# Cosine attention on one core: the norm sums of 36 pairs' Q taken by VectorE's statistics instruction, K scaled on GpSimd, a cubic in place of a quartic, and new engine orders

## The chip, the cores and the metric

One core of a Trainium2 chip runs the whole kernel. A core has five engines with an instruction queue each: TensorE (PE in the profile, its weight loads PEld), VectorE (DVE), ScalarE (ACT), GpSimd (POOL), and SyncE (SP), which here only issues DMAs. The metric is the device time of one execution in microseconds (us), the median of several runs. Every engine takes its instructions strictly in the order in which they were written for it, and a semaphore wait at the head of a queue holds back all that stands behind it.

## What is computed

For 8 batches x 12 heads, with 512 rows of 64 values each:

```python
Q_norm = Q / (np.linalg.norm(Q, axis=-1, keepdims=True) + 1e-10)
K_norm = K / (np.linalg.norm(K, axis=-1, keepdims=True) + 1e-10)
scores = np.einsum('bhqd,bhkd->bhqk', Q_norm, K_norm) / tau
weights = np.exp(scores - np.max(scores, axis=-1, keepdims=True))
weights = weights / (np.sum(weights, axis=-1, keepdims=True) + 1e-10)
return np.einsum('bhqk,bhkd->bhqd', weights, V)
```

With tau = 0.1 the scores lie between -10 and 10, so the kernel exponentiates without taking a maximum off. The sum of the weights is a 65th column of V that holds ones.

## The kernel before

The 96 heads are worked off as 48 **pairs** s = 0 to 47, two heads h each. Of Q and K a pair has 128 partitions x 8 rows (2 heads x 4 tiles t) x 64 values. Each pair goes through these steps; the name in capitals is the one under which the code registers the operation (`P.add`), and the line is the one that the profile shows:

- LD (L337), LV (L340): SP loads Q, K and V; a tile `qk` holds Q and K of a pair, 15 of them are in rotation.
- SQ (L366): GpSimd squares Q and K together, 128x1024, into `sq`, in bf16.
- SSQ (L396, L401) and RED (L410, L414, L418): the sum of 64 squares of each row. For the 40 pairs of `SUM_BOTH`, TensorE adds groups of columns with 16 matmuls by the identity, and VectorE reduces the 64 columns that remain to 16 sums in one instruction (L410). For the pairs of `BY_VECTOR` (35, 39, 43, 47), VectorE reduces all the squares itself with two 128x512 instructions (L418).
- NEW (L443, L447, L450): the reciprocal square root, by a bit trick and polynomial steps on small tiles, for a whole **group** of pairs at once (`GROUPS`: pairs 0 to 3 alone, 4 to 19 in groups of two, 20 to 47 in groups of four). Step 6 gives Q's factors, 7 K's factors for GpSimd, 8 K's factors for VectorE.
- SCL (L485): rows times factor, in bf16, into `qn`. Q is scaled on VectorE, K on VectorE for the 20 pairs of `K_ON_DVE` and on GpSimd for the others.
- TR (L494) and EVA (L512): TensorE transposes, VectorE copies the result from PSUM to `qt`. EVA is the last step ahead of the scores.
- SCO (L633) and EXP (L657): for each of 4 chunks c of 128 keys, TensorE computes 128x1024 scores into one of two PSUM buffers, and ScalarE takes their exponential into `et`. A score chunk must wait for the exponential of the chunk two before it.
- PV (L682), RCP (L701), NRM (L703), ST (L707): TensorE multiplies the weights by V (cast on GpSimd, VC, L665), VectorE takes the reciprocal of the 65th column and scales the output, SP stores it. The SSQ of a later pair uses a spare part of the same PSUM bank, between a pair's PV and its RCP.

Two chunks, (36, 3) and (45, 3) (`OFF`), don't go to ScalarE: VectorE cuts their scores (X, L573, L575) into a power of two and a rest, and GpSimd computes a polynomial of the rest (Y, L595, L596, L602, L603), 128x1024 at a time, six instructions each.

What sets the order: the table `ORDER` (from L814) lists for each engine, as numbers, the operations in the order in which the engine runs them. A number counts the `P.add` calls, which the code makes pair by pair. `Program.run` (L43) turns the needs of each operation into semaphore waits, and nothing is reordered on the chip. In this text RCP8.1 means RCP of pair 8, head 1.

The branch for `stats(s)` (L361, L378, L460) is in this version too, but `STATS_FROM = 99` turns it off. Its core:

```python
for h in range(2):
    rows = qk[iq][:, 0, h, :].rearrange("p (t d) -> p t d", t=NT)
    for t in range(0, NT, 2):
        last = e.bn_stats(out=st[...two groups of three...],
                          in_=rows[:, t : t + 2].rearrange("p t d -> p d t"))
```

One such instruction reads 128 values of f32 per partition, alternately from row t and from row t + 1, which lie 64 values apart, and gives count, mean and summed squared deviation of the even values (row t) and of the odd ones (row t + 1).

Of the kernel before, what the change touches and what calls it, by code (L numbers as in the profile page):

```python
# [108 lines left out]
def bass_cosine_similarity_attention_kernel(  # L109
# [200 lines left out]
    def stats(s):  # L310
        return s >= STATS_FROM and group[s] not in NORM_ON_ACT

# [10 lines left out]
    def pair(s):  # L323
# [6 lines left out]
        for w, x in ((0, Q), (1, K)):  # L330
            if s == 0:
                for h in range(2):
                    P.add(("LD", 0, w, h), "act" if w else "sp", "ldh", -1000 + h,  [],
                          lambda e, w=w, x=x, h=h: e.dma_start(out=qk[iq][:, w, h], in_=src(x, s)[:, h]), slot=f"head{w}_{h}")
                continue
            P.add(("LD", s, w), "sp", "ld1" if s == 1 else "ld", s, [*([("SCL", 0, w, 0), ("SCL", 0, w, 1), ("SQ", 0, w, 0), ("SQ", 0, w, 1)] if s == R_QK else [key("SCL", s - R_QK, w), *((squares(s - R_QK, w) if w or not stats(s - R_QK) else [("RED", s - R_QK, 0)]) if s >= R_QK else [])])],
                  lambda e, w=w, x=x: e.dma_start(out=qk[iq][:, w], in_=src(x, s)),  # L337
                  slot=f"first{s}_{w}" if s <= 3 else f"qk{iq}")
# [195 lines left out]
    def last_step(s, c):  # L534
        return 5 if (s, c) in OFF_ON_POOL + OFF_ON_BOTH else 4
# [18 lines left out]
    def poly(s, c, at):  # L554
# [4 lines left out]
        a0, a1, a2, a3, a4 = POLY_K if here else POLY  # L559
# [39 lines left out]
        if (s, c) in OFF_ON_POOL:  # L599
            k = cc ** 0.5  # L600
            steps = [("pool", "yt", mul(w, z, z)), ("pool", "ys", add(w, w, a1, k)),
                     ("pool", "ys", lambda e: e.tensor_scalar(out=z, in0=z, scalar1=a2 * cc, scalar2=a3 * cc, op0=ALU.mult, op1=ALU.add)),  # L602
                     ("pool", "yt", mul(w, w, w)), ("pool", "yt2", lambda e: e.tensor_tensor(out=w, in0=w, in1=z, op=ALU.add)),  # L603
                     ("pool", "yt3", mul(e_, w, p2))]
# [146 lines left out]
POLY = (-186.9751803485176, 100772.4799431421, -50373599.073513225, 207520169.07623482, 3.565140779347853e-11)  # L751
# [9 lines left out]
BY_VECTOR = (35, 39, 43, 47)  # L761
Q_ON_PE = ()
SUM_BOTH = (4, 5, 6, 7, 8, 9, 10, 11, 12, 13, 14, 15, 16, 17, 18, 19, 20, 21, 22, 23, 24, 25, 26, 27, 28, 29, 30, 31, 32, 33, 34, 36, 37, 38, 40, 41, 42, 44, 45, 46)
# [3 lines left out]
STATS_FROM = 99  # L767
# [8 lines left out]
JOINT_FROM = 0  # L776
OFF_ON_POOL = ((36, 3), (45, 3))
OFF_ON_BOTH = ()
X_ON_POOL = ()
K_ON_DVE = (1, 2, 3, 4, 9, 12, 15, 18, 21, 24, 27, 30, 33, 36, 39, 40, 42, 44, 46, 47)  # L780
# [29 lines left out]
def slack(s, most):  # L810
# [14 lines left out]
    ),  # L825
    "pool": (
# [7 lines left out]
    ),  # L834
    "dve": (
# [23 lines left out]
    ),  # L859
# [80 lines left out]
```

## Time and profile before

| what | value |
|---|---|
| median of 3 runs | 188.97 us (188.75 to 189.37) |
| profiled execution, first to last instruction (its span) | 186.8 us |
| what the median has beyond that span | 2.2 us |
| ScalarE (ACT) busy | 180.2 us, 210 instructions |
| VectorE (DVE) busy | 159.9 us, 523 instructions |
| GpSimd (POOL) busy | 165.7 us, 147 instructions |
| TensorE busy / weight loads busy | 179.5 us / 117.9 us, 3010 each |
| granted TensorE clock | 1.00 throughout |

The profile is that of one execution. "Busy" is the time in which at least one instruction of the engine runs; instructions of one engine can overlap, so on an engine whose instructions overlap the mean duration of one is more than the distance from one start to the next. Waits are attributed to what released them. The page gives for the profiled execution its span, no other time.

### The profile page before, as it was taken

Reading aid. Unit: us, or ns where it says so; the run is one execution under the profiler, and the core shown is the slowest. Engines: PE = TensorE matmul, PEld = TensorE weight load, DVE = VectorE, ACT = ScalarE, POOL = GpSimd, SP = SyncE. Lnnn points to the kernel's source line nnn. Section 1 sums busy time; section 2 is a strip of 40 time slices with the busy share of each in tenths; the row PEclk is TensorE's granted clock in tenths of the full one; section 3 lists DMA queues with packets and bytes.
Section 4 is the critical chain, followed back from the end, with each engine's and each line's share of the span. In section 5 each row is a group of like instructions: output and inputs, shape, how many; then the busy total and the mean of one; then the engine's idle time right before and its main releaser. Section 6 shows DMA issues by size and latency. Waiting matters only on the chain.

```text
span 186.8 us, 7242 instructions
## 1 busy us (share of the span) xinstructions
PE 179.5 (96%) x3010; PEld 117.9 (63%) x3010; DVE 159.9 (86%) x523; ACT 180.2 (96%) x210; POOL 165.7 (89%) x147
## 2 busy tenths in 40 slices
PE   7889999999999999999999999999999999998993
PEld 2456766666667666666676666766656566555653
DVE  2789998987987978979889988999999999998664
ACT  5799999999999999999999999999999999999992
POOL 3799999999989998999999899999999999907940
PEclk9999999999999999999999999999999999999999
DMA  5999999999999877999999999999798731113135
GB/s 158 354 349 351 349 358 329 288 351 364 370 376 369 283 245 230 309 303 307 312 379 367 328 371 335 319 312 298 241 303 294 239 105 56 60 56 116 60 112 168
DMA packets 52447, 50.79 MB, mean 272 GB/s; under 512 B 3136, under 2 KB 52416, under 8 KB 52416
## 3 DMA queue, kind: packets, MB, share of 16 engines
q1 hardware_dynamic: 51984, 50.02, 81.8%
q8 instruction: 23, 0.38, 0.8%
q10 hardware_dynamic: 432, 0.33, 0.5%
q14 instruction: 8, 0.07, 0.1%
HBM read 37.75 MB, written 12.58 MB: 269 GB/s over the span
## 4 chain that ended last, share of the span: by engine, by line
ACT 92%; PE 3%; DVE 2%; DMA 1%; POOL 0%; issue 0%; DVEq 0%
ACT et L657 91%; DMA qk<-in_K_dram 1%; PE oops L682 1%; PE scps L633 1%; DVE xs L260 1%; DVE ob L732 0%; POOL sq L256 0%; PE tps L283 0%; ACT ys L432 0%; DVE qn L273 0%; DVE ob L703 0%; PE oops L401 0%; ACT nps L435 0%; PE oops L281 0%; DVE rd L730 0%
## 5 line engine op out<-in xcount | busy, mean ns | idle before, releaser
L657 ACT ACTIVATE et<-scps 128x1024 bf16<-128x1024 f32 (+1 forms) x191 | 173.8, 1155 | 0.3 <-PE scps L633 0.3
L366 POOL TENSOR_TENSOR sq<-qk 128x1024 bf16<-128x1024 f32 x44 | 82.8, 1895 | 0.6 <-DMA qk<-in_K_dram 0.6
L633 PE MATMUL scps<-qt 64*128 64x512 bf16 x380 | 74.5, 386 | 2.2 <-ACT et L657 1.0
L682 PE MATMUL oops<-vb,et 128*128 128x65 bf16 x1504 | 75.8, 194 | 0.1
L682 PEld LDWEIGHTS oops<-vb,et 128*128 128x128 bf16 x1504 | 57.0, 98 | 27.7 <-issue 21.9
L485 DVE TENSOR_TENSOR qn<-qk,nps 128x512 bf16<-128x512 f32 x67 | 44.2, 678 | 0.7 <-ACT nps L435 0.6
L703 DVE TENSOR_TENSOR ob<-oops,rd 128x256 f32<-128x256 f32 x94 | 39.5, 422 | 1.7 <-DVE ys L447 0.2
L512 DVE COPY qt<-tps 128x1024 bf16<-128x1024 bf16 x47 | 32.3, 687 | 3.9 <-PE tps L494 3.0
L494 PE MATMUL tps<-ident,qn 128*128 128x128 bf16 x376 | 34.3, 220 | 0.6 <-DVE qn L485 0.6
L485 POOL TENSOR_TENSOR qn<-qk,rk 128x512 bf16<-128x512 f32 x27 | 28.1, 1045 | 2.6 <-DVE rk L443 1.7
L665 POOL TENSOR_SCALAR vb<-vf 128x512 bf16<-128x512 f32 x48 | 29.3, 629 | 0.2
L633 PEld LDWEIGHTS scps<-qt 64*128 64x128 bf16 x380 | 18.3, 92 | 16.5 <-ACT et L657 4.8
L396 PE MATMUL oops<-sq,ident 128*128 128x64 bf16 x640 | 27.6, 192 | 0.0
L494 PEld LDWEIGHTS tps<-ident,qn 128*128 128x128 bf16 x376 | 21.7, 98 | 9.4 <-issue 3.4
L396 PEld LDWEIGHTS oops<-sq,ident 128*128 128x128 bf16 x640 | 22.2, 97 | 6.1 <-issue 5.7
L701 DVE RECIPROCAL rd<-oops 128x4 f32<-128x4 f32 x94 | 16.5, 178 | 10.4 <-PE oops L682 5.2
L410 DVE TENSOR_REDUCE nps<-oops 128x16 f32<-128x64 f32 x40 | 8.7, 217 | 2.0 <-PE oops L396 2.0
L596 POOL TENSOR_TENSOR xw<-xz 128x1024 f32<-128x1024 f32 x2 | 3.8, 1895 | 5.6 <-DVE xz L575 5.6
L443 DVE SCALAR_TENSOR_TENSOR nps<-nps,ys 128x32 f32<-128x32 f32 (+3 forms) x45 | 7.9, 190 | 0.4
L195 PE MATMUL oops<-warm_in 128*128 128x512 bf16 x10 | 4.4, 631 | 1.0 <-DVE warm_in L199 1.0
L357 POOL TENSOR_TENSOR sq<-qk 128x512 bf16<-128x512 f32 (+1 forms) x5 | 4.6, 954 | 0.8 <-DMA qk<-in_K_dram 0.6
L418 DVE TENSOR_REDUCE nps<-sq 128x8 f32<-128x512 bf16 x8 | 5.3, 684 | 0.0
(64 smaller groups left out, 72.5 us busy)
## 6 DMA issues: line engine op xcount, KB each, us to landing
vf<-in_V_dram SPq DMA_DIRECT2D x48, 256.0 KB, 5.6
qk<-in_Q_dram SPq DMA_DIRECT2D x47, 256.0 KB, 4.4
qk<-in_K_dram SPq DMA_DIRECT2D x47, 256.0 KB, 5.8
out_dram<-ob SPq DMA_DIRECT2D x47, 256.0 KB, 3.8
qk<-in_Q_dram SPq DMA_DIRECT2D x2, 128.0 KB, 2.6
qk<-in_K_dram ACTq DMA_DIRECT2D x2, 128.0 KB, 2.8
out_dram<-ob SPq DMA_DIRECT2D x1, 128.0 KB, 1.9
out_dram<-ob SPq DMA_DIRECT2D x1, 64.0 KB, 1.8
```

The lines of the kernel that those rows point to most:

```text
L366: lambda e: e.tensor_tensor(out=sqf, in0=data, in1=data, op=ALU.mult))
L396: last = e.matmul(out=o_ps[bank][:, 320:384], lhsT=ident[:, :], rhs=sq[iqs][:, :, 4 * k : 4 * k + 4], start=(k == 0), stop=(k == 15), skip ...
L410: lambda e, bank=bank, dst=x2[:, :, c8 : c8 + 8]: e.tensor_reduce(out=dst, in_=o_ps[bank][:, 320:384].rearrange("p (w g e) -> p w g e", w= ...
L485: lambda e, w=w, r=r: e.tensor_tensor(out=qn[iqn][:, w].rearrange("p t h d -> p h t d"), in0=qk[iq][:, w].rearrange("p h (t d) -> p h t d" ...
L494: last = e.transpose(t_ps[:, w, t, :], qn[iqn][:, w, t].rearrange("p h d -> p (h d)"), ident[:, :])
L512: lambda e, ws=ws: e.tensor_copy(out=qt[iqt][:, ws, :, :].rearrange("p w t x -> p (w t x)"), in_=t_ps[:, ws, :, :].rearrange("p w t x -> p ...
L633: last = e.matmul(out=sc_ps[:, 2 * b + h, :], lhsT=qt[iqt][64 * h : 64 * h + 64, 1, c, :], rhs=qt[iqt][64 * h : 64 * h + 64, 0, :, :], sta ...
L657: lambda e, c=c, b=b, hs=hs: e.activation(out=et[iet][:, c, hs[0] : hs[-1] + 1, :], in_=sc_ps[:, 2 * b + hs[0] : 2 * b + hs[-1] + 1, :], f ...
L665: return e.tensor_scalar(out=out, in0=in_, scalar1=1.0, scalar2=1.0, op0=ALU.mult, op1=ALU.mult)
L682: last = e.matmul(out=o_ps[h][:, 65 * t : 65 * t + 65], lhsT=et[iet][:, c, h, 128 * t : 128 * t + 128], rhs=vb[:, iq, c, h, :], start=(i = ...
L701: lambda e, hs=slice(0, 2) if s in RCPJ else hs, grid=r_all: e.reciprocal(out=rd[io][:, hs, :], in_=grid[:, :, :, DIM]))
L703: lambda e, hs=hs, grid=grid: e.tensor_tensor(out=ob[io][:, hs], in0=grid[:, :, :, 0:DIM], in1=rd[io][:, hs, :].unsqueeze(3).to_broadcast( ...
```

## The change

- `stats(s)` becomes true for groups 8 to 18, that is pairs 12 to 47. For these 36 pairs GpSimd squares K alone (128x512, L363), VectorE runs four statistics instructions on the loaded Q (BN below), TensorE sums K's squares alone with 8 matmuls (L400 on), VectorE reduces them (L414), and each group has three more small VectorE steps ahead of NEW (-3, -2, -1), which make 64 x mean^2 + deviation out of the statistics. `SUM_BOTH` is cut to pairs 4 to 11, `BY_VECTOR` to none.
- `K_ON_DVE` is cut to pairs 1 to 4: the K of 16 more pairs is scaled on GpSimd, and step 8 goes where it existed for those.
- The polynomial has one degree less: GpSimd has five instructions for each of the two chunks instead of six. The two chunks are the same.
- Q and K of a tile `qk` get a semaphore each (`slot`). A later Q may be loaded over the old one when BN is done.
- All five lists of `ORDER` are new, ScalarE's by renumbering alone: its instructions and their order are the same. On SP some stores stand behind later loads (ST5 behind pair 17's loads; ST26 to ST28 behind pair 41's). `JOINT_FROM` has no effect, since `JOINT` is False.

```diff
@@ -308,7 +308,7 @@
     def stats(s):
-        return s >= STATS_FROM and group[s] not in NORM_ON_ACT
+        return group[s] in STATS
@@ -335,7 +335,7 @@
-                  slot=f"first{s}_{w}" if s <= 3 else f"qk{iq}")
+                  slot=f"first{s}_{w}" if s <= 3 else f"qk{iq}_{w}")
...
         if (s, c) in OFF_ON_POOL:
-            k = cc ** 0.5
-            steps = [("pool", "yt", mul(w, z, z)), ("pool", "ys", add(w, w, a1, k)),
-                     ("pool", "ys", lambda e: e.tensor_scalar(out=z, in0=z, scalar1=a2 * cc, scalar2=a3 * cc, op0=ALU.mult, op1=ALU.add)),
-                     ("pool", "yt", mul(w, w, w)), ("pool", "yt2", lambda e: e.tensor_tensor(out=w, in0=w, in1=z, op=ALU.add)),
-                     ("pool", "yt3", mul(e_, w, p2))]
+            steps = [("pool", "yt", mul(w, z, z)), ("pool", "ys", add(w, w, a1, cc)),
+                     ("pool", "ys", lambda e: e.tensor_scalar(out=z, in0=z, scalar1=a2, scalar2=1.0, op0=ALU.add, op1=ALU.mult)),
+                     ("pool", "yt", mul(w, w, z)), ("pool", "yt3", mul(e_, w, p2))]
...
-BY_VECTOR = (35, 39, 43, 47)
+BY_VECTOR = ()
-SUM_BOTH = (4, 5, 6, 7, 8, 9, 10, 11, 12, 13, 14, 15, 16, 17, 18, 19, 20, 21, 22, 23, 24, 25, 26, 27, 28, 29, 30, 31, 32, 33, 34, 36, 37, 38, 40, 41, 42, 44, 45, 46)
+SUM_BOTH = (4, 5, 6, 7, 8, 9, 10, 11)
-STATS_FROM = 99
+STATS = (8, 9, 10, 11, 12, 13, 14, 15, 16, 17, 18)
-JOINT_FROM = 0
+JOINT_FROM = 4
-K_ON_DVE = (1, 2, 3, 4, 9, 12, 15, 18, 21, 24, 27, 30, 33, 36, 39, 40, 42, 44, 46, 47)
+K_ON_DVE = (1, 2, 3, 4)
...
```

VectorE's new list from pair 8's copy to pair 12's, with the numbers replaced by names (g8.-3 is step -3 of NEW for group 8):

```
EVA8 BN12 RED11 RCP6.0 g7.0 NRM6.0 g7.1 BN13 RCP6.1 g7.2 g8.-3 NRM6.1 g7.5
EVA9 g7.3 g7.4 g8.-2 RED12 g7.6 g7.7 RCP7.0 SCL10.Q RCP7.1 SCL11.Q NRM7.1 NRM7.0 BN14
EVA10 g8.-1 BN15 RED13 RCP8.0 g8.0 NRM8.0 g8.1
EVA11 g8.2 BN17 g8.5 g9.-3 RCP8.1 g8.3 g8.4 g9.-2 NRM8.1 g8.6 g8.7 RCP9.0 SCL12.Q NRM9.0 RCP9.1 RED14 NRM9.1 g9.-1 SCL13.Q
EVA12
```

GpSimd's new list around the same place: `SCL9.K VC9 VC7 VC11 SQ12 SCL10.K SCL11.K SQ13 SQ16 VC10 VC12 SQ14 VC13 SCL12.K SQ15 SCL13.K`, and TensorE's: `SCO11.0 PV9.1 SCO11.1 TR12.0 TR12.1 SCO11.2` (PV shortened).

More of the change, by code (lines that the diff above doesn't have):

```diff
@@ L534, in last_step @@
     def last_step(s, c):
-        return 5 if (s, c) in OFF_ON_POOL + OFF_ON_BOTH else 4
+        return 4
     def exps(s, c):
@@ L558, in poly @@
         here = in_psum(s)
-        a0, a1, a2, a3, a4 = POLY_K if here else POLY
+        a0, a1, a2, a4 = POLY
         lift = LIFT_K if here else LIFT
@@ L750 @@
 LIFT = 71
-POLY = (-186.9751803485176, 100772.4799431421, -50373599.073513225, 207520169.07623482, 3.565140779347853e-11)
+POLY = (-131.77899651091911, 109622.99404139613, -167.5284161360313, -2.6307902185888065e-08)
 OFF = {(36, 3): (36, 36), (45, 3): (45, 45)}
```

160 rows, old and new, of the table ORDER are left out of this document.

## The prediction

> **What bounds the kernel now.** I read the page's busy times first, then the chain that ended last (its line by engine, and its long piece in order of time), then the table by stretches, then VectorE's timeline for start-to-start steps.
>
> ```profile
> span 186.8 us, 7242 instructions
> PE 179.5 (96%) x3010; PEld 117.9 (63%) x3010; DVE 159.9 (86%) x523; ACT 180.2 (96%) x210; POOL 165.7 (89%) x147
> ACT 92%; PE 3%; DVE 2%; DMA 1%; POOL 0%; issue 0%; DVEq 0%
> 7.52 0.33 PE scps L633
> 11.89 167.82 ACT et L657 x183
> 38.20:82.20 44.00, 43.96 (x792) 30.18 (x791) 37.69 (x140) 44.00 (x49) 42.22 (x34) 1.00 0.97 321
> 82.20:140.90 58.70, 58.45 (x1011) 39.06 (x1009) 53.91 (x165) 58.70 (x66) 57.76 (x50) 1.00 0.98 322
> 140.90:179.70 38.80, 37.05 (x586) 23.15 (x584) 34.38 (x100) 38.80 (x44) 32.38 (x26) 1.00 0.37 119
> ```
>
> From 11.89 to 179.71 the chain is ScalarE alone: 183 exponentials without a hole, 167.82 / 183 = 0.917 us each, 3.67 us per pair of four. The windows (columns: stretch, length, then busy time and count of PE, PEld, DVE, ACT, POOL) say the same: ACT is busy for all of 44.0, 58.7 and 38.8 us. So **ScalarE is the bound**, and 11.9 us ahead of it and 7.1 behind it (186.8 - 179.7) are the rest of the span. VectorE has room in the first window: 37.69 of 44.00 us.
>
> The change leaves ScalarE's list as it is: the same exponentials, and the same two chunks go round it. What the edits take from other engines is therefore worth nothing while ScalarE stays full. The question is only whether VectorE, which gets the new work, still delivers each pair's copy (EVA) in time. What it costs there is the start-to-start step, not the duration, since VectorE's instructions overlap. Its timeline (start, duration):
>
> ```profile
> 18.36 0.19 DVE L450 TENSOR_TENSOR nps<-nps,ys 128x32 f32<-128x32 f32 x1
> 18.46 0.68 DVE L512 COPY qt<-tps 128x1024 bf16<-128x1024 bf16 x1
> ...
> 36.16 0.68 DVE L512 COPY qt<-tps 128x1024 bf16<-128x1024 bf16 x1
> 36.76 0.68 DVE L485 TENSOR_TENSOR qn<-qk,nps 128x512 bf16<-128x512 f32 x1
> ...
> 102.94 0.21 DVE L443 SCALAR_TENSOR_TENSOR ys<-nps,ys 128x64 f32<-128x64 f32 x1
> 103.07 0.22 DVE L443 SCALAR_TENSOR_TENSOR nps<-nps,ts 128x64 f32<-128x64 f32 x1
> ...
> 106.82 0.18 DVE L701 RECIPROCAL rd<-oops 128x4 f32<-128x4 f32 x1 [0.25 <-PE oops L396]
> 106.92 0.20 DVE L410 TENSOR_REDUCE nps<-oops 128x16 f32<-128x64 f32 x1
> ...
> 109.31 0.42 DVE L703 TENSOR_TENSOR ob<-oops,rd 128x256 f32<-128x256 f32 x1
> 109.64 0.68 DVE L485 TENSOR_TENSOR qn<-qk,nps 128x512 bf16<-128x512 f32 x1
> ...
> 110.79 0.22 DVE L410 TENSOR_REDUCE nps<-oops 128x16 f32<-128x64 f32 x1
> 110.92 0.68 DVE L418 TENSOR_REDUCE nps<-sq 128x8 f32<-128x512 bf16 x1
> 111.51 0.68 DVE L512 COPY qt<-tps 128x1024 bf16<-128x1024 bf16 x1
> ...
> 165.29 0.69 DVE L573 TENSOR_SCALAR xp<-tps 128x512 int16<-128x512 f32 x1
> 166.01 0.69 DVE L575 SCALAR_TENSOR_TENSOR xz<-xp,tps 128x512 f32<-128x512 int16 x1
> ...
> 184.08 0.29 DVE L732 TENSOR_TENSOR ob<-tps,rd 128x128 f32<-128x128 f32 x1
> 184.29 0.28 DVE L732 TENSOR_TENSOR ob<-oops,rd 128x128 f32<-128x128 f32 x1
> ```
>
> Steps read off: EVA 36.76 - 36.16 = 0.60; NRM (256 values) 0.33; RED by L410 0.13; a 512-value reduce 111.51 - 110.92 = 0.59, and a scaling, also 512 values, the same 0.60; RCP 0.10; a NEW step 0.13 on 64 columns, 0.10 on 32; X 0.72; 128 values 0.21.
>
> **The price that decides: one statistics instruction.** No row shows one. It reads 128 f32 values per partition and runs without a wait behind its neighbour. From 512 values at 0.59 and 256 at 0.33, 256 values cost 0.26, so 128 come to 0.33 - 0.13 = 0.20; L732's pair, 128 values, has 0.21. I take **0.20**, the nearest rows in size. The ends: nothing to gain below 0.13, which is 128 values with no fixed part; above, 0.28 if the four don't overlap at all (L732's duration), and 0.33 if each value takes twice as long (256 values' step).
>
> The Trainium skill (VectorE: DVE Perf Modes, section "The DRAIN you can't avoid") says that the next VectorE instruction cannot start until the pipe is empty. By that rule the four would stand 0.28 apart, and the time would be that of the first rival below instead of the forecast's. The trace disagrees: the copy lasts 0.68, and the next instruction starts after 0.60.
>
> **The change part by part.** VectorE first, by the new list, in the two stretches that matter.
>
> *Pair 8's copy to pair 20's.* The list holds 12 EVA (7.2), 11 Q scalings (6.6), 24 NRM (7.9), 24 RCP (2.4), 15 RED (2.0), 14 BN of four (14 x 0.80 = 11.2), 52 NEW steps of small groups (5.2) and 11 of groups of four (1.4): **43.9 us**. ScalarE needs 48 x 0.917 = 44.0. So VectorE is full here, where it had over 6 us idle. It is this tight because the groups of two pay 11 NEW steps for two pairs, and because BN runs ahead: 14 pairs' statistics in 12 pairs' time. It starts with something in hand: pair 8's first exponential is the 30th of the 183, so due at 11.89 + 29 x 0.917 = 38.5, its copy starts at 36.16, and copy and scores need 0.68 + 0.33, about 1.0 with the waits between, so some 1 us.
>
> *Pair 20's copy to pair 37's.* 17 EVA, 18 scalings, 32 NRM, 32 RCP, 16 RED, 18 BN, 45 NEW and 4 X: 10.2 + 10.8 + 10.6 + 3.2 + 2.1 + 14.4 + 5.9 + 2.9 = **60.1 us** against 67 x 0.917 = 61.4. Behind that only 4 BN are left for ten pairs.
>
> So VectorE keeps up, with no more than about 1 us to lose in the first stretch. Its waits come on top. The longest kinds so far:
>
> ```profile
> DVE rd L701 <- PE oops L682: 5.2, 12, 1.2
> DVE rd L701 <- PE oops L396: 4.2, 11, 0.8
> DVE qt L512 <- PE tps L494: 3.0, 8, 0.9
> DVE nps L410 <- PE oops L396: 2.0, 6, 0.6
> ```
>
> These are waits of an engine that is ahead. A VectorE that is full reaches the same instructions later, when TensorE is done, so most of them go; what is late next is VectorE itself. I leave 1 to 1.5 us of them in the first stretch, which uses up what is in hand: **+0.3 us**.
>
> *GpSimd, TensorE, polynomial.* All cover, at nothing:
>
> ```profile
> L366 POOL TENSOR_TENSOR sq<-qk 128x1024 bf16<-128x1024 f32 x44 | 82.8, 1895 | 0.6 <-DMA qk<-in_K_dram 0.6
> L485 POOL TENSOR_TENSOR qn<-qk,rk 128x512 bf16<-128x512 f32 x27 | 28.1, 1045 | 2.6 <-DVE rk L443 1.7 <-DVE nps L443 0.7 <-PE tps L494 0.2
> L357 POOL TENSOR_TENSOR sq<-qk 128x512 bf16<-128x512 f32 x4 | 4.0, 1039 | 0.1
> L603 POOL TENSOR_TENSOR xw<-xw,xz 128x1024 f32<-128x1024 f32 x2 | 4.7, 2354 | 0.2
> L396 PEld LDWEIGHTS oops<-sq,ident 128*128 128x128 bf16 x640 | 22.2, 97 | 6.1 <-issue 5.7 <-POOL vb L665 0.2 <-POOL sq L366 0.2
> qk<-in_Q_dram SPq DMA_DIRECT2D x47, 256.0 KB, 4.4
> ```
>
> GpSimd: 36 squares shrink by 1.895 - 1.039 (-30.8 us), 16 K scalings come (+16.7), two polynomial instructions go (between -3.8 and -4.7; the product of two equal tiles becomes one of two different ones): 165.7 becomes about 147. It had no part in the chain, so nothing is gained; the polynomial ends 2 us earlier in chunks that ScalarE doesn't wait for. TensorE loses 256 - 32 = 224 of 640 + 48 sum matmuls; PE is full by its modelled busy time, but ScalarE never waited for it. The new wait is that TR of K needs GpSimd's 1.05 us scaling behind NEW step 7, where VectorE took 0.60. Behind a waiting TR stand the scores of the next chunk, and behind them ScalarE. For pair 12: pair 11's copy comes 10.1 us behind pair 8's in the list, at 46.3, step 7 another 2.5 us on, the scaling ends 1.3 later, at 50.1, the transpose at 50.4. The scores behind it belong to exponential 44 of the 183, due at 11.89 + 43 x 0.917 = 51.3, and take 0.33: free by half a microsecond.
>
> SP: BN12 reads Q straight from the load, 4.4 us after the issue, and the ring is 15 deep; stores that go behind loads have eight output buffers. Nothing. The head has GpSimd's memsets moved under the wait for K, and the tail swaps two stores: within 0.1 us.
>
> **The sum.** 186.8 + 0.3 = 187.1 for the span; with the 2.2 us that the median has beyond it, **189.3**.
>
> **The rivals.**
>
> *The statistics cost 0.28 to 0.29 each* (no overlap, or a dearer read). Place: VectorE between pair 8 and pair 37. From 0.22 on it decides, since 56 instructions x 0.02 = 1.1 us is all that is in hand. At 0.28 the first stretch is 56 x 0.08 = 4.5 longer, less 1, plus the waits; the second 72 x 0.08 = 5.8, less the room of 1.3: together +8, which ScalarE never gets back: **197**. Against it: all short rows overlap. For it: BN reads alternately from two rows 64 values apart, and no row of the trace reads SBUF like that. The Trainium skill (Vector Engine (DVE) Microarchitecture Reference, section "Measured stream behaviour on trn2") says that a port runs at full rate only on runs of two or more adjacent 4-byte words; a source that hops on every value took 1.73 instead of 1.05 ns per value, but one stream alternating between two distant regions ran at full rate. An estimate by its 1.73 is 0.29 per instruction, and by its exception 0.20; no run here shows which.
>
> *Twice the time per value*, 0.33: 56 x 0.13 - 1 + 72 x 0.13 - 1.3 = +14: **203**.
>
> *TensorE's queue stops at a TR* that waits for GpSimd's K, at the first pair of a group: 0.3 to 0.5 us at some of 11 places if step 7 slips by over half a microsecond: **190.5**. For it: GpSimd's scaling waits already show (2.6 us in the L485 row).
>
> *Head and tail gain* half a microsecond by the new orders, with nothing lost between: **188.3**. Against it: the ends of the chain keep their instructions.
>
> **How the numbers follow.** Forecast 55% (own range 188.6 to 190.6: from nothing lost to the first stretch late by 1.5), the 0.28 case 28%, the 0.33 case 10%, TensorE's queue 4%, the gain 3%. About 0.3% (0.57 us) is what a measurement of this kernel can tell from no change. Of the forecast's 55%, 36 lie within that, 18 above, 1 below. Faster 1 + 3 = 4%, same 36%, slower 18 + 28 + 10 + 4 = 60%. The range runs from 188.5 to 197.5: it leaves out the 0.33 case, the gain and the upper edge of the 0.28 case, under 2 in 10.
>
> **What would show it.** Right: ACT still one piece of about 167.8 us, DVE busy near 10 in every window from 36 to 80, four statistics rows 0.20 apart, POOL near 147. Wrong: statistics 0.28 apart or more, ACT waiting for scores whose copy (L512) came late, in pairs 12 to 22 first; or ACT waiting behind a TR (L494) that waits for POOL's L485.

## The result, and the profile after

The changed kernel takes 190.7 us (median of 4 runs, 190.31 to 192.1), the kernel before 188.99 beside it: a ratio of 1.0101, 95% interval 1.0064 to 1.0139. It is slower by 1.7 us. The forecast of 189.3 had the sign right, and the range of 188.5 to 197.5 holds the result, but the sum had 0.3 us of loss where 1.7 came.

The page of the profiled execution (its own time 190.84 us): busy times, the line of the chain by engine, and two groups.

```profile
span 189.0 us, 6973 instructions
PE 176.4 (93%) x2786; PEld 111.2 (59%) x2786; DVE 168.3 (89%) x669; ACT 180.4 (95%) x210; POOL 147.7 (78%) x161
ACT 73%; POOL 6%; SPq 6%; PE 5%; DMA 5%; DVE 2%; issue 2%; POOLq 1%; DVEq 0%
L655 ACT ACTIVATE et<-scps 128x1024 bf16<-128x1024 f32 (+1 forms) x191 | 174.3, 1192 | 2.6 <-PE scps L631 2.3
L383 DVE BATCH_NORM_STATS2 st<-qk 128x6 f32<-128x128 f32 x144 | 31.6, 283 | 0.9 <-DMA qk<-in_Q_dram 0.9
```

ScalarE has the same work (180.4 us busy, before 180.2), but the span is 2.2 longer, and the exponentials now wait 2.3 us for scores, at five places: one of 0.55 us at the very start, where the kernel before waits 0.32, and four where it ran in one piece. GpSimd is down to 147.7 us and TensorE by 224 matmuls, as the change says; neither bought anything. VectorE, the prediction's worry, is full in the two windows of before, and ScalarE is busy in all of both:

```profile
38.20:82.20 44.00, 42.39 (x690) 26.96 (x686) 42.37 (x202) 44.00 (x50) 35.13 (x41) 1.00 1.00 332
82.20:140.90 58.70, 56.19 (x885) 35.37 (x881) 57.15 (x231) 58.70 (x66) 46.89 (x56) 1.00 0.93 305
```

(DVE is the third column of busy time.) So the loss lies outside these windows. VectorE's timeline, start and duration, shows why it keeps up:

```profile
44.93 0.88 DVE L383 BATCH_NORM_STATS2 st<-qk 128x6 f32<-128x128 f32 x4
45.72 0.68 DVE L512 COPY qt<-tps 128x1024 bf16<-128x1024 bf16 x1
```

Four statistics instructions take 45.72 - 44.93 = 0.79, a step of 0.20 each at a duration of 0.283. ScalarE's timeline has three holes early on (each start is late by 0.1 to 0.2 us more than the hole, since an exponential of 1.02 us overlaps the next, 0.917 on), and another at the end, shown further down:

```profile
19.86 4.71 ACT L655 ACTIVATE et<-scps 128x1024 bf16<-128x1024 f32 x5
25.13 1.02 ACT L655 ACTIVATE et<-scps 128x1024 bf16<-128x1024 f32 x1 [0.55 <-PE scps L631]
26.37 2.85 ACT L655 ACTIVATE et<-scps 128x1024 bf16<-128x1024 f32 x3 [0.22 <-PE scps L631]
29.68 11.36 ACT L655 ACTIVATE et<-scps 128x1024 bf16<-128x1024 f32 x12 [0.46 <-PE scps L631]
```

Behind the first two holes stands TensorE, and behind TensorE GpSimd (two fences, one for each engine):

```profile
24.12 0.64 PE L396 MATMUL oops<-sq,ident 128*128 128x64 bf16 x16 [0.56 <-POOL sq L366]
25.71 0.30 PE L680 MATMUL oops<-vb,et 128*128 128x65 bf16 x4 [0.30 <-POOL vb L663]
30.42 0.40 PE L494 MATMUL tps<-ident,qn 128*128 128x128 bf16 x4 [0.23 <-POOL qn L485]
```

```profile
18.48 0.62 POOL L663 TENSOR_SCALAR vb<-vf 128x512 bf16<-128x512 f32 x1
20.82 1.39 POOL L663 TENSOR_SCALAR vb<-vf 128x512 bf16<-128x512 f32 x2 [1.71 <-DMA vf<-in_V_dram]
22.17 1.89 POOL L366 TENSOR_TENSOR sq<-qk 128x1024 bf16<-128x1024 f32 x1
24.02 1.04 POOL L485 TENSOR_TENSOR qn<-qk,rk 128x512 bf16<-128x512 f32 x1
25.03 0.63 POOL L663 TENSOR_SCALAR vb<-vf 128x512 bf16<-128x512 f32 x1
```

GpSimd's new list casts the V of pairs 4 and 5 directly behind that of pair 2. At 19.1 the V of pair 4 isn't there, and for 1.71 us all that follows stands behind it: the squares of pair 7, the scaled K of pair 5, the V of pair 3, and later (29.32) the scaled K of pair 6. TensorE's list has the sums of pair 7 ahead of SCO4.1, a product of pair 3 ahead of SCO4.2, and the transposes of pair 6 ahead of SCO5.3: these are the three rows of TensorE above, and EXP4.1, EXP4.2 and EXP5.3 start 0.74, 0.33 and 0.25 us late. Before, the squares of pair 7 stood in that place of GpSimd's list, and started at 20.07 instead of 22.17.

The third hole is of another kind. TensorE waits for nothing there; its new list has the last product of pair 3, the sums of pair 8 and four products of pair 4 ahead of SCO5.1 (the last row is SCO5.1 and SCO5.2), where the old one has the sums alone:

```profile
28.21 0.63 PE L396 MATMUL oops<-sq,ident 128*128 128x64 bf16 x16
28.68 0.64 PE L680 MATMUL oops<-vb,et 128*128 128x65 bf16 x16
29.25 0.61 PE L631 MATMUL scps<-qt 64*128 64x512 bf16 x4
```

The hole at the end is in front of pair 47's scores. TensorE, and the same place in the chain that ended last (there `POOLq L87` is the time of the polynomial's last step):

```profile
179.90 0.92 PE L680 MATMUL oops<-vb,et 128*128 128x65 bf16 x24
181.08 0.42 PE L680 MATMUL oops<-vb,et 128*128 128x65 bf16 x8 [0.26 <-POOL et L596]
181.43 0.60 PE L631 MATMUL scps<-qt 64*128 64x512 bf16 x4
```

```profile
176.47 2.35 POOL xw L596
178.86 2.17 POOLq L87
181.08 0.42 PE oops L680 x8
181.50 0.34 PE scps L631 x2
181.86 2.86 ACT et L655 x3
```

All eight products of pair 45, two of which need the polynomial, now stand ahead of SCO47.0.

To read all runs by one measure I compare starts of the same exponentials with those of the profiled kernel before: **head** is the delay at EXP2.1; **2-6**, **6-16** and **16-46** are what it grows by to EXP6.1, EXP16.0 and EXP46.0; **end** to the last exponential; **tail** from there to the end of the span. The changed kernel: head -0.12, 2-6 **+1.82**, 6-16 -0.13, 16-46 -0.02, end **+0.87**, tail -0.28: 2.15 between these two executions, where the medians differ by 1.7. A stage is read from one execution of each kernel.

### The profile page after: what moved, and what is told of

The parts are those of the page before. It is cut to its first block, busy times and chain, and to the rows that moved or that the text cites. A ratio compares the mean times of both kernels' runs of the same rounds, so it can differ in the third digit from the quotient of the medians.

```text
span 189.0 us, 6973 instructions
## 1 busy us (share of the span) xinstructions
PE 176.4 (93%) x2786; PEld 111.2 (59%) x2786; DVE 168.3 (89%) x669; ACT 180.4 (95%) x210; POOL 147.7 (78%) x161
## 4 chain that ended last, share of the span: by engine, by line
ACT 73%; POOL 6%; SPq 6%; PE 5%; DMA 5%; DVE 2%; issue 2%; POOLq 1%; DVEq 0%
ACT et L655 73%; DMA vf<-in_V_dram 5%; SPq L337 4%; POOL xw L596 2%; PE oops L680 2%; SPq L340 1%; PE scps L631 1%; POOLq L87 1%; POOL qn L485 1%; DVE xp L573 1%; DVE xz L575 1%; POOL vb L663 1%; PE tps L494 1%; POOL xw L595 1%; POOL xz L601 1%
## 5 line engine op out<-in xcount | busy, mean ns | idle before, releaser
L680 PE MATMUL oops<-vb,et 128*128 128x65 bf16 x1504 | 72.6, 194 | 0.7 <-POOL vb L663 0.3
L680 PEld LDWEIGHTS oops<-vb,et 128*128 128x128 bf16 x1504 | 55.4, 98 | 28.1 <-issue 18.2
L485 POOL TENSOR_TENSOR qn<-qk,rk 128x512 bf16<-128x512 f32 x43 | 44.3, 1043 | 18.0 <-DVE rk L443 18.0
L363 POOL TENSOR_TENSOR sq<-qk 128x512 bf16<-128x512 f32 x36 | 37.2, 1040 | 6.3 <-DMA qk<-in_K_dram 5.0
L485 DVE TENSOR_TENSOR qn<-qk,nps 128x512 bf16<-128x512 f32 x51 | 33.9, 676 | 1.2 <-ACT nps L435 1.1
L383 DVE BATCH_NORM_STATS2 st<-qk 128x6 f32<-128x128 f32 x144 | 31.6, 283 | 0.9 <-DMA qk<-in_Q_dram 0.9
L401 PE MATMUL oops<-sq,ident 128*128 128x64 bf16 x336 | 16.8, 193 | 0.6 <-POOL sq L363 0.3
L401 PEld LDWEIGHTS oops<-sq,ident 128*128 128x128 bf16 x336 | 12.6, 98 | 4.8 <-issue 2.1
L366 POOL TENSOR_TENSOR sq<-qk 128x1024 bf16<-128x1024 f32 x8 | 15.1, 1893 | 0.2 <-DMA qk<-in_K_dram 0.2
L414 DVE TENSOR_REDUCE nps<-oops 128x8 f32<-128x64 f32 x38 | 8.1, 216 | 0.0
L396 PE MATMUL oops<-sq,ident 128*128 128x64 bf16 x128 | 5.3, 192 | 0.6 <-POOL sq L366 0.6
```

The source lines that it names most:

```text
L363: lambda e: e.tensor_tensor(out=sqf[:, 8 * DIM :], in0=data[:, 8 * DIM :], in1=data[:, 8 * DIM :], op=ALU.mult))
L383: last = e.bn_stats(out=st[:, g % R_X, c8 + 4 * h + t : c8 + 4 * h + t + 2, :].rearrange("p g x -> p (g x)"), in_=rows[:, t : t + 2].rearr ...
L401: last = e.matmul(out=o_ps[bank][:, at : at + 64], lhsT=ident[:, :], rhs=sq[iqs][:, 8 * w : 8 * w + 8, 8 * k : 8 * k + 8], start=(k == 0), ...
L485: lambda e, w=w, r=r: e.tensor_tensor(out=qn[iqn][:, w].rearrange("p t h d -> p h t d"), in0=qk[iq][:, w].rearrange("p h (t d) -> p h t d" ...
L680: last = e.matmul(out=o_ps[h][:, 65 * t : 65 * t + 65], lhsT=et[iet][:, c, h, 128 * t : 128 * t + 128], rhs=vb[:, iq, c, h, :], start=(i = ...
```

## The experiments

Operations are written by name, lists are cut to the place that changes.

**First four: which of the two places, and does it give the time back?** Theory A is as above; B says that VectorE is a limit of its own that the early delay hides.

GpSimd's list in the changed kernel:

```diff
-SQ6 VC2 VC4 VC5 SQ7 SCL5.K VC3 SQ8 SQ9 SCL6.K VC6 SCL7.K SQ10
+SQ6 VC2 SQ7 VC4 VC3 SCL5.K SQ8 SQ9 SCL6.K VC5 VC6 SCL7.K SQ10
```

> The changed kernel with one stretch of GpSimd's order as it was: the V casts of pairs 4 and 5 no longer stand ahead of SQ7, pair 5's scaled K and the V cast of pair 3. Theory A (those two casts wait for V's load and hold the three operations behind them; the scores of pairs 4 and 5 come late, and ScalarE keeps the 1.7 us to the end): EXP of pairs 6 to 46 start 1.5 to 1.8 us earlier than in the changed kernel, time 189.0 (188.8 to 189.3). Theory B (VectorE, busy for 42.4 of 44.0 us and 57.2 of 58.7, is a limit of its own, and the early shift only gave it the time): the exps of pairs 6 to 8 come early, but ScalarE then waits for scores between pairs 13 and 37; less than 0.8 us comes back, time 189.9 to 190.7.

Measured: 189.98 us (ratio 1.0053, 1.0023 to 1.0083). The stage 2-6 shrinks from 1.82 to 0.35, as A says; what stays is the third hole, in front of EXP5.1. But the median falls by less than half of 1.7 and lies in the range of B: the head costs 0.53, 6-16 0.26, the end 0.88. The intervals of this ratio and of the changed kernel's overlap, so the time alone doesn't show the gain.

The same edit the other way round, alone in the kernel before:

```diff
-SQ6 VC2 SQ7 VC4 VC3 SCL5.K SQ8 SQ9 SCL6.K SCL7.K VC5 SQ10
+SQ6 VC2 VC4 VC5 SQ7 SCL5.K VC3 SQ8 SQ9 SCL6.K SCL7.K SQ10
```

> The kernel before with nothing but that stretch of GpSimd's order taken from the changed kernel: V casts of pairs 4 and 5 directly behind that of pair 2. Theory A: the whole early loss without statistics instructions, without K scaled elsewhere, without the cubic: +1.5 to +1.8 us, time 190.6 (190.3 to 190.9). Theory B: the order of GpSimd alone costs nothing or little where VectorE has room: 189.0 to 189.4.

Measured: 189.76 us (9 runs, 189.14 to 191.93; ratio 1.0047, 1.0014 to 1.0079): slower, by half of what I expected. Its profiled run is the slowest of the nine (191.93). In it the head costs 1.65, the stage 2-6 1.66, all else nothing, and GpSimd shows the same wait:

```profile
20.50 0.63 POOL L665 TENSOR_SCALAR vb<-vf 128x512 bf16<-128x512 f32 x1
22.87 1.37 POOL L665 TENSOR_SCALAR vb<-vf 128x512 bf16<-128x512 f32 x2 [1.74 <-DMA vf<-in_V_dram]
```

TensorE's list at the end of the changed kernel, alone (e3) and with the casts put back (e4):

```diff
-SCO46.3 PV45 (eight) SCO47.0 SCO47.1 PV46 (eight) SCO47.2 SCO47.3
+SCO46.3 SCO47.0 SCO47.1 PV45 (eight) PV46 (eight) SCO47.2 SCO47.3
```

> The changed kernel with all products of pair 45 with V behind the scores of pair 47's second chunk on TensorE, so that these scores no longer stand behind products that wait for the polynomial of pair 45. Theory A: the last 0.8 us of ScalarE's delay goes, 0.5 to 0.8 us come back, time 190.0 (189.8 to 190.3). Rival C (the scores were late by themselves, or what is moved behind comes late at the end of the kernel and gives the gain away): within 0.2 us of the changed kernel, 190.5 to 190.8.

> Both moves together in the changed kernel. Theory A: the two delays are separate and add: 190.7 - 1.7 - 0.6 = 188.4 (188.0 to 188.8), a little below the kernel before. Theory B and C: 189.7 to 190.7. If the delay at the end only came from the early one (everything late by 1.7 us), this is the same as the first run with the casts put back.

Measured: 191.6 us (1.0160, 1.0118 to 1.0202) and 191.89 us (1.0161, 1.0128 to 1.0194): both above every range expected and, by the medians, slower than the changed kernel: the edit was wrong. All 16 products of pairs 45 and 46 now stand between SCO47.1 and SCO47.2, and the second eight wait for their PSUM bank; SCO47.0 waits too, for the copy of pair 47. No product waits for the polynomial any more, which ends at 180.59. From e3 (the first two rows are SCO47.0 and SCO47.1):

```profile
180.31 0.39 PE L631 MATMUL scps<-qt 64*128 64x512 bf16 x2 [0.79 <-DVE qt L512]
180.92 0.39 PE L631 MATMUL scps<-qt 64*128 64x512 bf16 x2 [0.21 <-ACT et L655]
181.24 1.15 PE L680 MATMUL oops<-vb,et 128*128 128x65 bf16 x32
183.00 1.15 PE L680 MATMUL oops<-vb,et 128*128 128x65 bf16 x32 [0.61 <-DVE ob L701]
184.09 0.61 PE L631 MATMUL scps<-qt 64*128 64x512 bf16 x4
```

The end costs 2.16 instead of 0.87 in both. But e3 gave something else: it has the early casts, and its GpSimd waits only 0.64 us for the V of pair 4, with a stage 2-6 of 0.74. The wait isn't the same in every execution.

**Then: mend all places, load VectorE further, and the polynomial alone.**

```diff
 GpSimd: as the first experiment
 TensorE:
-SCO5.0 PV3.13 SSQ8 PV4.0 (four) SCO5.1 SCO5.2 TR6 SSQ9 PV4.10 SCO5.3
+SCO5.0 SSQ8 SCO5.1 PV4.0 (four) SCO5.2 TR6 SCO5.3 PV4.10 SSQ9
-SCO10.3 PV9.03 SSQ14.1 SCO11.0 PV9.1 (four) SCO11.1
+SCO10.3 PV9.03 SCO11.0 PV9.10 PV9.11 SSQ14.1 SCO11.1 PV9.12 PV9.13
-SCO46.3 PV45 (eight) SCO47.0 SCO47.1 PV46 (eight) SCO47.2 SCO47.3
+SCO46.3 PV45.0 (three) SCO47.0 PV45.10 PV45.11 SCO47.1 PV45 (three) SCO47.2 PV46.0 (four) SCO47.3 PV46.1 (four)
```

Ahead of SCO5.0, the products of pair 3 and the transposes of pair 5 are in the old order again too, and SCO6.0 stands ahead of the last three products of pair 4; the transposes of pair 7 stay ahead of SCO6.1, where the old list has them behind it.

> The changed kernel, all of its operations kept, with four places of its orders as in the kernel before: GpSimd's V casts of pairs 4 and 5; TensorE's products and sums around the scores of pairs 4 and 5 (SCO5.1 and SCO5.3 ahead of products of pair 4); the sums of K for pair 14 behind the scores SCO11.0; and the end (SCO47.0 and SCO47.1 ahead of the last products of pair 45, SCO47.2 and SCO47.3 ahead of those of pair 46). Theory A' (mended after the first four runs: the loss is TensorE's head of list, at four places, each holding one score behind something that is late or long): ScalarE's delay against the kernel before stays within 0.2 us from EXP1 to EXP47, time 188.5 to 189.1. Theory B (VectorE full, or late sums, are a limit of their own): the delay comes back at other places between pairs 11 and 47; 189.7 to 190.7.

Measured: 191.53 us (1.0120, 1.0099 to 1.0142): the theory fell, or the mending did. Stage 2-6 is down to 0.29, all of it now at EXP6.1, behind the transposes of pair 7; but 6-16 costs 0.70, and end and tail 0.68 and 0.93. VectorE's timeline shows one cause:

```profile
47.87 0.88 DVE L383 BATCH_NORM_STATS2 st<-qk 128x6 f32<-128x128 f32 x4 [0.43 <-DMA qk<-in_Q_dram]
...
50.35 0.18 DVE L699 RECIPROCAL rd<-oops 128x4 f32<-128x4 f32 x1 [0.58 <-PE oops L401]
```

RCP9.0 waits for the sums SSQ14.1 in the same PSUM bank, which I had moved back. Behind it stands the scaling of pair 12's Q, for this wait the transposes of pair 12, and behind these, on TensorE, SCO11.2: EXP11.2 starts 0.55 us late.

A fifth statistics instruction per pair, its result unused:

```diff
+                        if h:
+                            e.bn_stats(out=extra[:, s, :], in_=rows[:, 0:2].rearrange("p t d -> p d t"))
                         for t in range(0, NT, 2):
```

> The kernel with the mended orders and a fifth statistics instruction for each of the 36 pairs (the first half of a head's values read again, its result unused): VectorE has 36 x 0.20 = 7.2 us more, 2.4 us of them between the copies of pairs 8 and 20 and 3.2 us between those of 20 and 36. Prediction's reading (VectorE has about 1 us in hand in each of the two stretches, then it sets the pace): 2.4 - 1.0 + 3.2 - 1.0 and what follows, 192.5 (191.5 to 194). Rival (the copies run far ahead of the scores, so that VectorE's room is larger than its idle time in a window tells): 188.7 to 189.8.

Measured: 193.27 us (1.0220, 1.0184 to 1.0256), 1.7 more than the run beside it for 7.2 us more work, in the range of the prediction's reading. But the stages put the loss in one place only: 6-16 grows by 1.15, all later ones by 0.1. VectorE's row and its second window:

```profile
L384 DVE BATCH_NORM_STATS2 extra<-qk 128x6 f32<-128x128 f32 x36 | 10.0, 278 | 0.0
```

```profile
82.20:140.90 58.70, 55.95 (x878) 35.15 (x879) 58.70 (x250) 58.69 (x64) 46.33 (x55) 1.00 0.93 307
```

VectorE is busy for 58.70 of 58.70 us, and ScalarE takes 0.4 us longer from pair 20 to pair 37 than in the run beside it, of which 0.1 is left at pair 46: the copies come just in time.

The cubic alone in the kernel before (its steps as in the change's diff):

> The kernel before with the cubic polynomial alone (one GpSimd multiplication of 2.1 us less in each of two chunks). Y45 then ends at about 177.6 instead of 179.75. Theory A' (a late Y45 costs only where scores stand behind its products; before they were not late): 188.7 to 189.0, no change. Rival D (the end of GpSimd's polynomial sets the last scores before too): 0.3 us or more faster, 188.0 to 188.6.

Measured: 189.15 us (0.9997, 0.9976 to 1.0018), the head 0.18 and every later stage 0.02 or less: nothing, as forecast.

**Then: mend the mending, with and without the early part.** Two edits on the run with mended orders:

```diff
 VectorE:
-EVA11 g8.2 BN17 g8.5 .. g8.7 RCP9.0 SCL12.Q
+EVA11 g8.2 g8.5 .. g8.7 SCL12.Q BN17 RCP9.0
-RCP44.0 NRM44.0 RCP44.1 NRM44.1 EVA47 RCP45.1 RCP45.0 ..
+RCP44.0 NRM44.0 EVA47 RCP44.1 NRM44.1 RCP45.0 NRM45.0 RCP45.1 ..
 TensorE:
+TR47.1 next to TR47.0; SCO46.2 ahead of PV44.11; SCO47.1 behind PV45.12
```

> The kernel with the mended orders and two more edits of order. On VectorE between the copies of pairs 11 and 12, the scaling of pair 12's Q and the Newton steps of group 8 now stand ahead of the statistics of pair 17 and of RCP9.0, which waited 0.43 and 0.59 us there. At the end, both engines' lists agree (VectorE: EVA47 ahead of RCP44.1, then pair by pair and head by head; TensorE: the transposes of pair 47 together, the scores of pair 47 ahead of the products that wait). Theory E (formed after the mended orders: two limits of about 1.5 us side by side, the early waits of TensorE and, hidden behind them, VectorE's list from the copy of pair 8 to that of pair 13, which runs as many statistics ahead as it passes pairs; mending one shows the other): the delay at EXP13.0 falls from +1.3 to +0.3, the end adds at most 0.3; time 189.3 (188.9 to 189.8), within 0.3% of the kernel before. Rival (VectorE's list is too long there whatever its order, only the waits change places): delay at EXP13.0 stays over 1.0, time 190.2 to 191.

> The same two edits (VectorE between pairs 11 and 12, and the end) in the changed kernel, with GpSimd's and TensorE's orders of the first 14 pairs as the change has them. Theory E: the early waits hold ScalarE back by 1.7 us by EXP5.3 as in the changed kernel, VectorE's gain is hidden behind them, and only the end's 0.8 us come back: delay +1.6 at EXP13.0 and to EXP46, time 189.9 (189.6 to 190.3). Rival (the early waits matter only together with VectorE's): as the run beside it, 189.3.

Measured: 190.96 us (1.0086, 1.0057 to 1.0114) and 191.62 us (1.0124, 1.0083 to 1.0165; 190.6 to 193.46, the profiled run is the lowest): the first in its rival's range, the second above both. In e8 the delay at EXP13.0 is 1.16 us, over 1.0 as the rival said, but 0.47 of it is the head: without the head it fell from 1.16 to 0.69, and EXP11.2 is 0.10 late instead of 0.55. The gain is gone again at EXP15.0 (6-16 costs 0.78): sums of K ahead of pair 15's scores wait 0.70 us for squares, and GpSimd had waited 0.53 for a load ahead of them. The end costs 0.03 in both, but the tail 1.14 and 0.76, where the changed kernel had 0.87 and -0.28: together no gain. In e9's profile stage 2-6 costs 0.45 and 6-16 nothing, although its early lists are the changed ones, because V came only 0.34 us late:

```profile
20.20 1.39 POOL L663 TENSOR_SCALAR vb<-vf 128x512 bf16<-128x512 f32 x2 [0.34 <-DMA vf<-in_V_dram]
```

**Is it VectorE after all?** The statistics of pairs 12 to 21 read 16 values of each row instead of 64, in the run with everything mended and in the changed kernel:

```diff
-in_=rows[:, t : t + 2].rearrange("p t d -> p d t"))
+in_=rows[:, t : t + 2, 0 : 16 if s <= 21 else DIM].rearrange("p t d -> p d t"))
```

> The run before last (all orders mended, on VectorE and at the end too) with VectorE made lighter in one place: the statistics of pairs 12 to 21 read a quarter of each row (16 of 64 values, so the norms of these pairs' Q leave out three quarters of the sum); no instruction and no order changes. If the step of a statistics instruction follows its elements, each pair costs VectorE 0.3 to 0.5 us less, 3 to 5 us in all between the copies of pairs 8 and 16. Theory F (the loss is VectorE's list in that stretch: ten pairs' statistics fall between the copies of pair 8 and pair 14, six pairs; the early waits of TensorE only hid it): ScalarE's delay between EXP2.1 and EXP16.0 falls from +0.9 and more to +0.2, the time to 189.7 (189.3 to 190.1; the end still costs about 0.6). Rival (TensorE's order, GpSimd's squares or the loads set the delays there): the delay at EXP16.0 stays at +0.8 or more, time 190.5 to 191.

> The changed kernel with the same lighter statistics for pairs 12 to 21 (same part of the sum left out) and its own orders. Theory F: the early waits still hold ScalarE back by 1.6 us before VectorE's stretch begins, so no more than 0.3 us comes back: 190.4 to 190.8, delay at EXP16.0 +1.4 to +1.7. Rival (VectorE's list is the only limit and the early waits are made up later): delay at EXP16.0 under 0.5, time 189.5.

Measured: 191.28 us (1.0103, 1.0074 to 1.0133) and 190.66 us (1.0094, 1.0076 to 1.0112). Groups by form, from the first of the two:

```profile
L383 DVE BATCH_NORM_STATS2 st<-qk 128x6 f32<-128x128 f32 x104 | 22.7, 282 | 0.0
L383 DVE BATCH_NORM_STATS2 st<-qk 128x6 f32<-128x32 f32 x40 | 4.7, 179 | 1.1 <-DMA qk<-in_Q_dram 1.0
```

VectorE has 4 us less to do, and nothing comes back: theory F fell with the first of the two. The second came out as F says, but it would also if VectorE's load played no part. Both profiled runs are the slowest of their six. The changed kernel with lighter statistics has the same stages as without (1.84, -0.14, -0.01, 0.87, -0.27) and the same early wait:

```profile
21.53 1.39 POOL L663 TENSOR_SCALAR vb<-vf 128x512 bf16<-128x512 f32 x2 [1.74 <-DMA vf<-in_V_dram]
```

The mended one even loses 1.57 in 6-16, since sums of K stand ahead of pair 15's scores and wait for squares, and GpSimd had waited 1.66 us for a load ahead of them:

```profile
65.82 0.41 PE L401 MATMUL oops<-sq,ident 128*128 128x64 bf16 x8 [1.36 <-POOL sq L363]
66.06 0.41 PE L680 MATMUL oops<-vb,et 128*128 128x65 bf16 x8
66.40 0.39 PE L631 MATMUL scps<-qt 64*128 64x512 bf16 x2
```

**Last: bring the loads forward.** On the run with everything mended, SyncE's list, and the end's products as before:

```diff
-LV11 ST3 ST4 LD12 LD13 LD14 LV12
+LV11 LD12 LD13 LD14 ST3 ST4 LV12
```

> The kernel with all orders mended (VectorE's and the end's too) and two more edits. On SyncE the loads of Q and K of pairs 12, 13 and 14, which need no buffer back, stand ahead of the stores of pairs 3 and 4; in the changed kernel SyncE waited for those stores' data from 27.7 to 33.3 us with the DMA engines under-used. And the last products of pair 47 and the last normalisations are in the order of the kernel before. Theory G (formed after VectorE was relieved without gain: statistics and squares of K run further ahead than the sums did, so they meet the loads; VectorE's and GpSimd's waits for loads between 37 and 66 us are what TensorE's list, with the sums of K ahead of scores, hands to ScalarE): the loads of pairs 12 to 18 land some 3 us earlier, statistics and squares wait for none of them, ScalarE's delay grows by less than 0.3 us between EXP2.1 and EXP16.0, and the end costs under 0.3: 189.4 (189.0 to 189.8). Rival (VectorE's list is too full in that stretch, loads or not): delay still grows by 0.7 or more, time 190.2 to 191.

Measured: 190.83 us (1.0084, 1.0053 to 1.0115; 189.4 to 191.5). ScalarE's part is 0.29, 0.23, -0.08 and 0.03 in the stages, 0.47 in all: the end as expected, the 0.52 up to EXP16.0 more than the expected 0.3, with 0.29 of it still at EXP6.1. From 30 to 70 us neither statistics nor squares waited for a load. But the tail costs 1.23 and the profiled run's head 0.86, so the time didn't follow and lies in the rival's range. No version beat the kernel before.

## Why the prediction was right or wrong

- **ScalarE is the bound, its list stays.** Right, and it is why nothing taken off GpSimd or TensorE paid: e7 takes 2 us off the polynomial for no gain. "One piece of 167.8 us" was wrong: it has four waits for scores now, 1.8 us in all.
- **A statistics instruction at 0.20.** Right: 0.20 to the next start, 0.283 long. Both rivals with a dearer one (28% and 10%) fell with it. With 32 values the step is (44.70 - 44.31) / 4 = 0.10 (rows below), so a value costs (0.20 - 0.10) / 96, about 1.0 ns. That is no more than in the prediction's rows that read without a hop (0.26 us for 256 values), so the hop between two rows costs nothing.

```profile
44.31 0.46 DVE L383 BATCH_NORM_STATS2 st<-qk 128x6 f32<-128x32 f32 x4
44.70 0.67 DVE L512 COPY qt<-tps 128x1024 bf16<-128x1024 bf16 x1
```

  The Trainium skill (Vector Engine (DVE) Microarchitecture Reference, section "Measured stream behaviour on trn2") gives 1.04 ns per value and some 75 ns per instruction; an estimate from these is 0.208 and 0.108. The trace agrees within 0.01, and with the page's exception for a single read stream that alternates between two regions. The rule of the empty pipe, which the prediction takes from the Trainium skill (VectorE: DVE Perf Modes, section "The DRAIN you can't avoid"), has an exception there that the prediction leaves out: a next instruction that is not held starts earlier. The 0.20 at a duration of 0.283 agrees with that.
- **VectorE's lists of 43.9 and 60.1 us, about 1 us in hand in each.** The first was right in size: 2.4 us more (the fifth instruction) cost 1.15, so some 1.2 was in hand even in the run with mended orders. The second was too small: 3.2 us more cost 0.4 there, and 0.1 is left of it at pair 46. The 0.3 us that the sum puts here didn't come: ScalarE lost nothing in 6-16 (-0.13). So it is luck that the sign and the range came true; the loss comes from terms that the sum has at nothing. That VectorE's load sets the early loss is ruled out by e11.
- **"GpSimd, TensorE, polynomial. All cover, at nothing."** This step failed. It priced what GpSimd and TensorE have to do in all, and one new wait, the scaled K of pair 12. It didn't walk the new lists of the first ten pairs, where two casts stand ahead of their data, and where TensorE's own work stands ahead of scores. The rival "TensorE's queue stops at a TR" (190.5, given 4%) was the right kind of event, TensorE's list stopping behind a late GpSimd; a TR did stop so, at pair 6 (0.23 us), but sums and a product cost more, and the reason was another. In the four profiled runs with the early casts and the new lists, waits for V of 1.71, 1.74, 0.64 and 0.34 us go with losses of 1.82, 1.84, 0.74 and 0.45 in stage 2-6; in the old lists (e2), 1.74 goes with 1.66. Not all of it is the casts': the seven runs of the changed kernel with the casts put back still lose 0.28 to 0.35, without a wait for another engine, in front of EXP5.1 (e1, e4) or EXP6.1 (the others), where TensorE's list has products or transposes ahead of scores. The medians move less, by 0.9 us (e2) and about 0.6 (e1 against the changed kernel, each beside its own kernel before); that the wait differs between executions would explain it, but only one execution of each has a trace.
- **"Head and tail within 0.1."** Wrong by 0.59: end 0.87 less tail 0.28. X45 starts at 168.84 instead of 165.29, while ScalarE is 1.7 late, so X45 has lost 1.85 us of its lead; the polynomial, 2 us shorter, ends 1.27 later, and pair 47's scores stand behind its products. This loss of lead is 1.81 to 1.86 us in all eleven runs with the new VectorE order, whether VectorE has 7.2 us more to do (e6) or 4 less (e11), so it isn't VectorE's load. The new list puts X45 behind a normalisation of pair 40 and parts it by others, where the old one has its first half ahead of them; that this place is the reason wasn't tried alone. That moving the scores ahead, with VectorE's order of the end, takes the hole away is shown (0.03 in e8, e9 and e12); that it then costs as much or more in the tail, too.

Open: why V's load came 0.3 us late in some executions and 1.7 in others; and the tail of the runs with a mended end: in e12 the span ends 3.5 us behind the last normalisation, before 2.3, and SyncE's first store of pair 47 took 1.14 us to issue where it took 0.34 before. That the late store of pair 46 is the reason wasn't tried.

## What to carry to other kernels

When an edit comes with new instruction orders, walk the new list of every engine from the first instruction, and ask of each one moved forward when its data lands and what stands behind it: here two casts of 0.6 us, moved ahead of a load, cost more than 36 pairs of new VectorE work. An engine that is busy for all of a window can still be harmless when its results come in time; test it by adding work (e6) and by taking work away (e11) before blaming it. Mending an order by hand moves the wait more often than it removes it, so compare stage by stage, not only times.

## What the runs showed of the hardware beyond that

The load of pair 4's V (256 KB) took 7.0 to 8.6 us from issue to landing in the 14 profiled runs, whose heads are nearly the same; where its cast stood ready, the wait was 0.34 to 1.74 us. The start of the work varied by as much (head -0.12 to 1.65 us). An order that leaves a load no slack turns that scatter into time.
